# Second expert mixture: 64-row second blocks in float32 on two column halves of the matrix array

## The chip, the cores and the metric

The kernel runs on one core of a Trainium2 chip. The core has a matrix engine (TensorE, PE in the rows), VectorE (DVE), ScalarE (ACT), GpSimd (POOL) and SyncE (SP), which issues loads, and 16 DMA engines. The metric is the device time of one execution in microseconds (us), as the median of several runs. Lower is better.

## The reference, cut to what matters

A first transformer block is followed by a second one. The second ends in a mixture of 64 experts, of which each of the 1024 tokens takes 8, plus one shared expert:

```python
def moe_ffn(h, w_router, router_bias, w_gate, w_up, w_down, ws_gate, ws_up, ws_down):
    ...                                   # scores, the 8 experts of a token, their weights wts
    def block_ffn(args):                  # one block of rows xb of one expert e
        xb, e = args
        return (jax.nn.silu(xb @ w_gate[e]) * (xb @ w_up[e])) @ w_down[e]
    ...                                   # every row scaled by its wts and summed per token
    shared = (jax.nn.silu(xt @ ws_gate) * (xt @ ws_up)) @ ws_down
    return (routed + shared).reshape(B, S, D)
```

`w_gate[e]` and `w_up[e]` are 1024 x 256, `w_down[e]` is 256 x 1024, all float32: 3 MB an expert, 192 MB in all. They are read once.

## The kernel before

`experts` (L1389) runs a list of blocks. A block is up to 128 token rows of one expert. In the second mixture `moe2` (L2530) makes the list: five blocks of the shared expert, then the 64 routed experts, ranked by how many tokens they got, and three more shared blocks. `CAPS2` (L2528) gives the places an expert has by its rank: 4 experts have 224 rows (blocks of 128 and 96), 8 have 192 (128 and 64), 20 have 176 (128 and 48), and 32 have 128, one block. Ranks i and 63 - i follow each other, so that the stage is 32 *triples*: a first block of 128 rows, a second block, and the one block of a small expert.

There are two ways to multiply. For an expert of one block (`whole`) the loaded float32 weights are the moving operand as they lie in their place `raw`, and TensorE runs them as float32 (L1477, one matmul instruction in the program, two in the trace). For an expert of two blocks the weights are first split by `wsplit` (L1437) into a high part `gh`/`dh` and a rest `gl`/`dl`, in six pieces; a piece is a ScalarE copy and a VectorE subtraction (L247, L253). Each product is then three cheaper passes, `gh*xh`, `gl*xh`, `gh*xl` (`mm3`, L271 to L273). The stationary operand is the transposed block of rows, so that a block of R rows uses R of the array's 128 columns, and 512 weight columns stream by.

For each block the loop at the end of `experts` writes, in this order: the gate and up products into `gups`; up to three pieces of the next split; the activation (`act`: `th` on ScalarE, `hh` twice on VectorE); the down products `yps` of the block before (`down`), whose rows are scaled and added to the output in memory by an indirect DMA (`acc_d<-y`); the rest of the pieces; the transposes `tp` of the block after the next; the transpose `hT` of this block's activation; and a few small matmuls `tab` (L1492), which turn a one-hot matrix `oh` into the row numbers and weights of a later block. No scheduler moves these: each engine takes its instructions in the order written.

Weights are loaded in thirds (gate and up in two, down in one) of 1 MB into a pool of `RAW2 = 7` places `raw`. The load of a third is issued by SP when the third seven before it is free:

```python
            while len(raw) < min(3 * len(keys) if ready[0] else 3, freed[0] + RAW):
```

A third of a split expert is free once its two pieces are made (L1450), a third of a whole expert once its matmuls have run. `gh` and `gl` have two buffers of two tiles each, `dh` and `dl` one. The first mixture uses the same function with blocks of 96 rows and its own pools. `LEAD2` (L2617) says at which of the first blocks the pieces of the first routed expert stand; four of its six subtractions may go to GpSimd (L1448), as only the first two experts of the list are allowed to.

Of the kernel before, what the change touches and what calls it, by code (L numbers as in the profile page):

```python
# [231 lines left out]
class Body:  # L232
# [1156 lines left out]
    def experts(self, cx, blocks, xsrc, wsrc, acc_d, C, route, pre=None, fin=None, whole=lambda key: False):  # L1389
# [15 lines left out]
                keys.append(b[2])  # L1405
        uses = {k: sum(b[2] == k for b in blocks) for k in keys}
        last_of = {b[2]: n for n, b in enumerate(blocks)}
        Wt = {}

        RAW = self.RAW1 if pre else self.RAW2  # L1410
# [25 lines left out]

        def wsplit(i):  # L1437

            gh, gl = [[wp.tile([128, 2048], F32R, name=f"{n}{a}") for a in range(2)] for n in ("gh", "gl")]
            Wt[keys[i]] = W = [list(zip(gu(gh), gu(gl))), None]  # L1440
            for q in range(6):
                if q == 4:
                    dh, dl = [wp.tile([128, 2048], F32R, name=n, bufs=self.DBUFS[n0 > 0]) for n in ("dh", "dl")]
                    W[1] = list(zip(down_(dh), down_(dl)))
                c = slice(q % 2 * 1024, q % 2 * 1024 + 1024)
                h, lo = (gh[q // 2], gl[q // 2]) if q < 4 else (dh, dl)
                self.split(raw[3 * i + q // 2][:, c], h[:, c], lo[:, c],
                           lo_eng="pool" if i < 2 and q not in (self.LOD if i else self.LOD0)[n0 > 0] else "dve")  # L1448
                if q % 2:
                    free(3 * i + q // 2)  # L1450
                yield

# [17 lines left out]
        def products_(out, pairs, start=True, stop=True):  # L1470
# [5 lines left out]
            for i, (x, w) in enumerate(pairs):  # L1476
                nc.tensor.matmul(out, x, w, start=start and i == 0, stop=stop and i == len(pairs) - 1, **kw)  # L1477

        idx, ohs, tab = {}, {}, {}

        def onehot(n, oh=None):
            r, off = blocks[n][:2]
            oh = ohs[n] = ep.tile([128, 8, C], BF, name="oh") if oh is None else oh
            nc.vector.tensor_tensor(oh, self.slot_r[:, None, off:off + C].to_broadcast([128, 8, C]),
                                    self.pos[:, :, r:r + 1].to_broadcast([128, 8, C]), op=OP.is_equal)

        def tabmm(n, first, a=0, b=6):
            if n == first and a == 0:
                tab[0] = p1.tile([128, 8, 6], F32, name="tab")
            oh = ohs.pop(n) if b == 6 else ohs[n]  # L1490
            for t in range(8):
                nc.tensor.matmul(tab[0][:C, n - first, a:b], oh[:, t], self.cols[:, t, blocks[n][0], a:b],  # L1492
                                 start=n == first and t == 0 and a == 0, stop=t == 7, skip_group_check=True)

        def tabfin(first, size, a=0, b=6):
            s = (slice(0, C), slice(0, size))
            if a == 0:
                tab[1] = ep.tile([128, 8, 6], F32, name="tb")
            tb = tab[1]
            nc.vector.tensor_copy(tb[s][:, :, a:b], tab[0][s][:, :, a:b])  # L1500
            if a:
                w = idx[first][3]
                nc.vector.tensor_tensor(w[s], tb[s][:, :, 3], tb[s][:, :, 4], op=OP.add)
                nc.vector.tensor_tensor(w[s], w[s], tb[s][:, :, 5], op=OP.add)
                return
            gi, si = [ep.tile([128, 8], I32, name=n, bufs=4) for n in ("gi", "si")]
            w, e = [ep.tile([128, 8], F32, name=n, bufs=4) for n in ("wsl", "emp")]
            nc.vector.scalar_tensor_tensor(e[s], tb[s][:, :, 0], 128.0, tb[s][:, :, 1], op0=OP.mult, op1=OP.add)
            nc.vector.tensor_copy(gi[s], e[s])
            nc.vector.tensor_scalar(w[s], tb[s][:, :, 2], -1.0, 1.0, op0=OP.mult, op1=OP.add)  # L1510
            nc.vector.scalar_tensor_tensor(si[s], w[s], self.spare[:C], e[s], op0=OP.mult, op1=OP.add)
            if b == 6:
                nc.vector.tensor_tensor(w[s], tb[s][:, :, 3], tb[s][:, :, 4], op=OP.add)
                nc.vector.tensor_tensor(w[s], w[s], tb[s][:, :, 5], op=OP.add)
            for j in range(size):
                R = blocks[first + j][3]
                idx[first + j] = (gi[:R, j:j + 1], si[:R, j:j + 1], w[:R, j:j + 1], w)


        todo = {}  # L1520
# [38 lines left out]
        def trans(n):  # L1559
            if n >= N:  # L1560
                return
            xg, R = XG.pop(n), blocks[n][3]
            ps = p1.tile([128, 2, 512], F32, name="tp")
            for k in range(8):
                nc.tensor.transpose(ps[:, k // 4, (k % 4) * R:(k % 4) * R + R], xg[:R, k * 128:k * 128 + 128],  # L1565
                                    self.ident[:R, :R])
            pv = ps[:, :, :4 * R].rearrange("p a (k c) -> p a k c", k=4)
            v = lambda z: z.rearrange("p (a k) c -> p a k c", a=2)
            if whole(blocks[n][2]):
                x = ep.tile([128, 8, C], F32, name="x", tag="xh")[:, :, :R]  # L1570
                nc.scalar.activation(v(x), pv, AF.Copy)
                X[n] = [x[:, k] for k in range(8)]
                return
            xh, xl = [ep.tile([128, 8, C], F32R, name=n_)[:, :, :R] for n_ in ("xh", "xl")]
            nc.scalar.activation(v(xh), pv, AF.Copy)  # L1575
            nc.vector.tensor_tensor(v(xl), pv, v(xh).bitcast(F32), op=OP.subtract)  # L1576
            X[n] = [(xh[:, k], xl[:, k]) for k in range(8)]
# [3 lines left out]
        def gate_up(n, mid=None):  # L1581
            key, R = blocks[n][2:]
            ps = pg.tile([128, 512], F32, name="gups")
            ops = list(zip(X.pop(n), Wt[key][0]))
            if mid:
                products_(ps[:R], ops[:4], stop=False)
                mid()
                products_(ps[:R], ops[4:], start=False)
            else:
                products_(ps[:R], ops)  # L1590
            Hs[n] = ps
            if whole(key) and last_of[key] == n:
                free(3 * keys.index(key), 3 * keys.index(key) + 1)

        def act(n):
            ps, R = Hs[n], blocks[n][3]
            th = ep.tile([128, 256], F32, name="th")
            hh = ep.tile([128, 256], F32, name="hh")
            nc.scalar.activation(th[:R], ps[:R, 0:256], AF.Tanh, scale=0.5)  # L1599
            nc.vector.scalar_tensor_tensor(hh[:R], th[:R], 1.0, ps[:R, 0:256], op0=OP.add, op1=OP.mult)  # L1600
            nc.vector.tensor_tensor(hh[:R], hh[:R], ps[:R, 256:512], op=OP.mult)
            Hs[n] = hh

        def h_trans(n):
            hh, R = Hs[n], blocks[n][3]
            ps = p1.tile([128, 2, C], F32, name="hT")[:, :, :R]
            for k in range(2):
                nc.tensor.transpose(ps[:, k], hh[:R, k * 128:k * 128 + 128], self.ident[:R, :R])
            if whole(blocks[n][2]):
                h = ep.tile([128, 2, C], F32, name="hT", tag="hTh")[:, :, :R]  # L1610
                nc.scalar.activation(h, ps, AF.Copy, scale=0.5)
                Hs[n] = [h[:, k] for k in range(2)]
                return
# [6 lines left out]
        def down(n):  # L1620
# [2 lines left out]
            h, (key, R) = Hs.pop(n), blocks[n][2:]  # L1623
            while piece(keys.index(key)):
                pass
            if n < N - 1 or not fin:
                ps = p1.tile([128, 1024], F32, name="yps")
                ps = [ps[:, q * 512:q * 512 + 512] for q in range(2)]
            else:
                ps = [pg.tile([128, 512], F32, name="gups") for q in range(2)]  # L1630
# [84 lines left out]
        transposes(0 if not n0 else 1)  # L1715

        first_of = {b[2]: n for n, b in reversed(list(enumerate(blocks)))}
        plan, since = {}, 0
        for i, key in enumerate(keys[1:], 1):
            if whole(key):  # L1720
                continue
            if i > 1 or not n0:
                w = range(since, first_of[key])
                for q in range(6):
                    plan.setdefault(w[q * len(w) // 6], []).append((i, q))
            since = last_of[key]
        if n0:
            plan |= self.LEAD2
        for n in range(N):
            key = blocks[n][2]  # L1730
            ki = keys.index(key)
# [176 lines left out]
        return f  # L1908

    CAP1 = 96  # L1910
    RAW1, RAW2 = 7, 7
    DBUFS = 2, 1
    START, ORDER = (1, 1, 2, 0), "oswsSSx"
    YACT = 5
# [610 lines left out]
        yield  # L2525


    CAPS2 = [(4, 224), (8, 192), (20, 176), (32, 128)]  # L2528

    def moe2(self, rt):  # L2530
        nc, tc, IN = self.nc, self.tc, self.IN
# [13 lines left out]
        R = {}  # L2545
        blocks = [(None, t, "shared", C) for t in range(8 - self.NT)]
        for i in range(E // 2):
            for r in (i, E - 1 - i):
                blocks += [(r, o, r, min(C, cap[r] - o)) for o in range(0, cap[r], C)]
        blocks += [(None, t, "shared again", C) for t in range(8 - self.NT, 8)]  # L2550
        ws = self.wsrc("_2")
# [41 lines left out]
        def norms():  # L2593
            with tc.tile_pool(reuse_waits="tile", name="c2", bufs=2) as ep:
# [18 lines left out]
    NT = 3  # L2613
    ROUTE = {(-1, 0): 2, (-1, 1): 1, (-1, 2): 1, (-1, 3): 1, (0, 0): 1, (0, 1): 2, (0, 3): 1, (1, 1): 1, (1, 2): 1,
             (1, 3): 1, (2, 1): 1, (2, 2): 1, (5, 3): 1}

    LEAD2 = {2: [(1, 0), (1, 1)], 3: [(1, 2), (1, 3)], 5: [(1, 4), (1, 5)]}  # L2617

    def run(self):
        tc, nc = self.tc, self.nc  # L2620
# [88 lines left out]
```

## Time and profile before

| | us |
|---|---|
| median of 3 runs | 3308.56 (3307.82 to 3311.86) |
| the profiled execution | 3307.24 |
| its span in the trace | 3305.3 |
| TensorE busy | 3000.4 (91%) |
| VectorE / ScalarE / GpSimd busy | 2045.1 / 1394.6 / 1022.6 |
| mean granted TensorE clock | 0.952 |

The trace is of one execution. Busy time is the time in which an engine had an instruction under way; the ends of matmuls are modelled, so a TensorE that is busy throughout may still hold small gaps, and the distance from one start to the next is the surer price. The second mixture's routed experts lie from about 2240 us to 3226 us. The DMA share is the mean busy share of the core's 16 DMA engines.

### The profile page before, as it was taken

The page shows a single profiled execution, that of the slowest core. Times are in us where ns is not written, and L with a number is a line of the kernel's source. Part 1 is how long each engine was busy: PE and PEld are TensorE (multiplying, and loading weights), DVE is VectorE, ACT ScalarE, POOL GpSimd, SP SyncE. Part 2 cuts the span into 40 slices and gives each one's busy share as a digit, 9 for nine tenths or more (in the row PEclk, how much of TensorE's full clock was granted, in tenths as well). Part 3 has the DMA queues.
Part 4 walks back from the last instruction along what each step waited for, and adds up shares of the span by engine and source line. Part 5 has one row for each costly group of instructions (what it writes and reads, how often), then busy time and mean ns, then how long its engine had stood idle before and what let it go on. Part 6 is the DMA issues. An engine that isn't in the chain of part 4 may idle for free.

```text
span 3305.3 us, 43066 instructions
## 1 busy us (share of the span) xinstructions
PE 3000.4 (91%) x16001; PEld 2322.3 (70%) x16001; DVE 2045.1 (62%) x3146; ACT 1394.6 (42%) x2096; POOL 1022.6 (31%) x682
## 2 busy tenths in 40 slices
PE   5999999988888978998699999779999999999994
PEld 4778887987777876666588888756666666666663
DVE  5554651667777658998545665466655555555546
ACT  3332331536666326676434334423433333333332
POOL 0000000236777323563111331133333233333323
PEclk9999999998999988999899998889999999999997
DMA  3112120453332448999501004448999999999993
GB/s 111 64 58 76 64 86 8 134 169 82 90 86 75 160 167 274 345 346 348 179 29 37 26 4 138 147 157 248 289 288 301 280 279 297 276 281 297 282 275 131
DMA packets 225254, 577.17 MB, mean 175 GB/s; under 512 B 22421, under 2 KB 104005, under 8 KB 225013
## 3 DMA queue, kind: packets, MB, share of 16 engines
q1 hardware_dynamic: 188240, 445.42, 38.6%
q0 software_dynamic: 36368, 128.88, 16.3%
q8 instruction: 128, 2.10, 0.3%
q14 instruction: 86, 0.70, 0.1%
q10 hardware_dynamic: 432, 0.06, 0.0%
HBM read 468.90 MB, written 105.33 MB: 174 GB/s over the span
## 4 chain that ended last, share of the span: by engine, by line
PE 48%; DVE 13%; DMA 6%; issue 4%; ACT 3%; POOL 1%; SPq 0%; another core or an unknown queue 0%; DVEq 0%; POOLq 0%; ACTq 0%
PE gups L1477 7%; PE gups L273 4%; PE gups L271 4%; PE gups L272 4%; PE yps L1477 3%; PE tp L1565 2%; DVE gl L253 2%; PE yps L273 2%; PE yps L271 2%; PE yps L272 2%; PE mm L2196 2%; PE mm L2198 2%; PE mm L2197 2%; PE o L969 2%; PE mm L272 1%
## 5 line engine op out<-in xcount | busy, mean ns | idle before, releaser
L1648 POOL DMA_INDIRECT acc_d<-y,si x96 | 179.7, 1872 | 643.8 <-DVE y L1645 605.2
L271 PE MATMUL gups<-gh,xh 128*96 128x512 f32 (+3 forms) x832 | 344.0, 413 | 1.3 <-ACT xh L1575 0.9
L272 PE MATMUL gups<-gl,xh 128*96 128x512 f32 (+3 forms) x832 | 334.4, 402 | 11.6 <-DVE gl L253 11.6
L273 PE MATMUL gups<-gh,xl 128*96 128x512 f32 (+3 forms) x832 | 334.8, 402 | 0.4 <-DVE xl L1576 0.4
L271 PE MATMUL mm<-uh,wh 128*128 128x512 f32 x640 | 253.7, 396 | 10.8 <-ACT t L505 8.8
L273 PE MATMUL mm<-uh,wl 128*128 128x512 f32 x640 | 252.4, 394 | 0.0
L272 PE MATMUL mm<-ul,wh 128*128 128x512 f32 x640 | 251.7, 393 | 0.0
L1645 DVE TENSOR_SCALAR y<-yps,wsl 128x512 f32<-128x512 f32 (+3 forms) x123 | 91.9, 747 | 239.7 <-ACT y L1643 239.7
L1477 PE MATMUL gups<-raw,x 128*128 128x512 f32 x512 | 228.0, 598 | 0.0
L1599 ACT ACTIVATE th<-gups 128x256 f32<-128x256 f32 (+1 forms) x136 | 51.7, 380 | 412.7 <-PE gups L273 241.5
L253 POOL TENSOR_TENSOR pl<-raw,ph 128x1024 fp32r<-128x1024 f32 (+7 forms) x128 | 203.5, 1608 | 71.4 <-ACT ph L247 36.8
L1643 ACT ACTIVATE y<-yps,wsl 48x512 f32<-48x512 f32 (+2 forms) x128 | 87.7, 685 | 317.7 <-PE yps L273 218.2
L253 DVE TENSOR_TENSOR gl<-raw,gh 128x1024 fp32r<-128x1024 f32 x183 | 218.9, 1238 | 3.4 <-ACT gh L247 3.2
L247 ACT ACTIVATE gh<-raw 128x1024 fp32r<-128x1024 f32 x188 | 188.0, 1057 | 2.0 <-DMA raw<-in_w_up_dram 1.6
L272 PEld LDWEIGHTS gups<-gl,xh 128*96 128x96 f32 (+3 forms) x832 | 139.9, 168 | 65.0 <-issue 12.8
L273 PEld LDWEIGHTS gups<-gh,xl 128*96 128x96 f32 (+3 forms) x832 | 138.8, 167 | 60.8 <-DVE xl L1576 1.1
L271 PE MATMUL yps<-dh,hTh 128*96 128x512 f32 (+3 forms) x412 | 176.2, 428 | 3.8 <-ACT et L2506 2.3
L271 PEld LDWEIGHTS gups<-gh,xh 128*96 128x96 f32 (+3 forms) x832 | 139.3, 167 | 54.0 <-ACT xh L1575 1.2
L1477 PEld LDWEIGHTS gups<-raw,x 128*128 128x128 f32 x512 | 94.7, 190 | 108.8 <-issue 107.1
L273 PE MATMUL yps<-dh,hTl 128*96 128x512 f32 (+3 forms) x412 | 162.7, 395 | 0.0
L272 PE MATMUL yps<-dl,hTh 128*96 128x512 f32 (+3 forms) x412 | 162.1, 394 | 0.0
L1600 DVE SCALAR_TENSOR_TENSOR hh<-th,gups 128x256 f32<-128x256 f32 (+1 forms) x136 | 56.6, 416 | 163.3 <-ACT th L1599 162.4
(672 smaller groups left out, 8010.3 us busy)
## 6 DMA issues: line engine op xcount, KB each, us to landing
raw<-in_w_down_dram SPq DMA_DIRECT2D x78, 1024.0 KB, 8.5
raw<-in_w_gate_dram SPq DMA_DIRECT2D x154, 512.0 KB, 5.3
raw<-in_w_up_dram SPq DMA_DIRECT2D x154, 512.0 KB, 9.2
w<-in_w_in_dram SPq DMA_DIRECT2D x20, 1024.0 KB, 5.3
b<-in_w_gate_dram SPq DMA_DIRECT2D x38, 512.0 KB, 10.6
b<-in_w_up_dram SPq DMA_DIRECT2D x38, 512.0 KB, 12.5
b<-in_w_down_dram SPq DMA_DIRECT2D x18, 1024.0 KB, 12.8
w<-in_w_in_dram SPq DMA_DIRECT2D x20, 512.0 KB, 4.6
```

What stands on the lines that cost most here:

```text
L247: nc.scalar.activation(hi, src, AF.Copy)
L253: e.tensor_tensor(lo, src, hi.bitcast(F32), op=OP.subtract)
L271: nc.tensor.matmul(out, lh, rh, start=start and i == 0, stop=False, **kw)
L272: nc.tensor.matmul(out, lh, rl, start=False, stop=False, **kw)
L273: nc.tensor.matmul(out, ll, rh, start=False, stop=stop and i == n - 1, **kw)
L969: nc.tensor.matmul(O[h][a // 512][:, a % 512:a % 512 + b - a], v, p[:, sl], start=kt == 0 and i == 0, stop=kt == (7 if a >= 512 else 3) an ...
L1477: nc.tensor.matmul(out, x, w, start=start and i == 0, stop=stop and i == len(pairs) - 1, **kw)
L1565: nc.tensor.transpose(ps[:, k // 4, (k % 4) * R:(k % 4) * R + R], xg[:R, k * 128:k * 128 + 128], self.ident[:R, :R])
L1643: nc.scalar.activation(y[:R, 0:512], ps[0][:R], AF.Copy, scale=w)
L1645: nc.vector.tensor_scalar(y[:R, 512:1024], ps[1][:R], w, None, op0=OP.mult)
L1648: nc.gpsimd.indirect_dma_start(out=acc_d, out_offset=bass.IndirectOffsetOnAxis(ap=si, axis=0), in_=y[:R], in_offset=None, compute_op=OP.add)
L2196: nc.tensor.matmul(out, lh, rh, start=(i == 0), stop=False)
```

## The change

Second blocks of 64 rows (`half`) get a third way to multiply. The rows' transposed block is placed twice in the array, in columns 0 to 63 and 64 to 127 (`tile_position`). For gate and up each half streams 256 of the 512 weight columns (128 of gate, 128 of up), for down 512 of the 1024, all in float32 from `raw`. The outputs of the two halves lie on partitions 0 to 63 and 64 to 127. The activation then works on 128 x 128, its transpose is one instruction, and the `tab` matmuls of such a block run once for each half, since the row weights are needed on both. `CAPS2` gives 28 experts 192 places, so that 28 second blocks have 64 rows and none has 48. The raw thirds of such an expert are free only after its second block's matmuls; `RAW2` is 11, and `gh`, `gl` have one buffer instead of two. The one-block expert of a pair now comes first in the list, the pieces of a split may begin right after the last block that uses the split before, and `LEAD2` is gone.

```diff
+        split_to = {b[2]: n for n, b in enumerate(blocks) if b[0] is None or b[3] != 64}
...
-            gh, gl = [[wp.tile([128, 2048], F32R, name=f"{n}{a}") for a in range(2)] for n in ("gh", "gl")]
+            gh, gl = [[wp.tile([128, 2048], F32R, name=f"{n}{a}", bufs=self.DBUFS[n0 > 0]) for a in range(2)]
+                      for n in ("gh", "gl")]
...
-                if q % 2:
+                if q % 2 and last_of[keys[i]] == split_to[keys[i]]:
                     free(3 * i + q // 2)
...
+        def half(n):
+
+            return blocks[n][0] is not None and blocks[n][3] == 64
+
+        def products2(ps, xs, ws):
+
+            for i, (x, w) in enumerate(zip(xs, ws)):
+                for h in range(2):
+                    nc.tensor.matmul(ps[64 * h:64 * h + 64], x, w(h), start=i == 0, stop=i == len(xs) - 1,
+                                     skip_group_check=True, tile_position=(0, 64 * h))
...
+            W = 64 if half(n) else C
+            nc.vector.tensor_tensor(oh[:, :, :W], self.slot_r[:, None, off:off + W].to_broadcast([128, 8, W]),
+                                    self.pos[:, :, r:r + 1].to_broadcast([128, 8, W]), op=OP.is_equal)
...
+                for h in range(2 if half(n) else 1):
+                    p, kw = (slice(64 * h, 64 * h + 64), dict(tile_position=(0, 64 * h))) if half(n) else (slice(C), {})
+                    nc.tensor.matmul(tab[0][p, n - first, a:b], oh[:, t, :p.stop - (p.start or 0)],
...
+            if half(n):
+                j = 3 * keys.index(key)
+                products2(ps[:, 0:256], X.pop(n), [lambda h, w=w: w[:, :, 128 * h:128 * h + 128]
+                                                   for w in gu([raw[j], raw[j + 1]])])
+                Hs[n] = ps
+                if last_of[key] == n:
+                    free(j, j + 1)
+                return
...
+            if half(n):
+                ps = p1.tile([128, 1024], F32, name="yps")[:, 0:512]
+                j = 3 * keys.index(key) + 2
+                products2(ps, h, [lambda q, w=w: w[:, q * 512:q * 512 + 512] for w in down_(raw[j])])
+                if last_of[key] == n:
+                    free(j)
...
-        plan, since = {}, 0
+        plan, since = {}, split_to[keys[0]] if n0 else 0
...
+            w = range(since, first_of[key])
+            if n0 and i > 2 and len(w) > 2:
+                w = w[1:]
+            for q in range(6):
+                plan.setdefault(w[q * len(w) // 6], []).append((i, q))
+            since = split_to[key]
...
-    RAW1, RAW2 = 7, 7
+    RAW1, RAW2 = 7, 11
...
-    CAPS2 = [(4, 224), (8, 192), (20, 176), (32, 128)]
+    CAPS2 = [(4, 224), (28, 192), (32, 128)]
...
-            for r in (i, E - 1 - i):
+            for r in (E - 1 - i, i):
```

TensorE in a triple before, from the end of a first block to the small expert's products. `gups` are gate and up products, `yps` down products, `tp` and `hT` transposes; the last number pair is the shape of the output; rows left out repeat the pattern.

```order
L1608 MATMUL hT<-ident,hh 128x128 x2
...
L273 MATMUL gups<-gh_21295,xl 64x512
L271 MATMUL yps<-dh,hTh 128x512
L272 MATMUL yps<-dl,hTh 128x512
L273 MATMUL yps<-dh,hTl 128x512
...
L1565 MATMUL tp<-ident,xg 128x128 x8
...
L1608 MATMUL hT<-ident,hh 128x64 x2
L1477 MATMUL gups<-raw,x 128x512 x8
L271 MATMUL yps<-dh,hTh 64x512
```

The same stretch after the change:

```order
L1643 MATMUL hT<-ident,hh 128x128 x2
L1490 MATMUL gups<-raw,x 64x256 x16
L271 MATMUL yps<-dh,hTh 128x512
L272 MATMUL yps<-dl,hTh 128x512
L273 MATMUL yps<-dh,hTl 128x512
...
L1584 MATMUL tp<-ident,xg 128x128 x8
...
L1638 MATMUL hT<-ident,hh 128x128
L1480 MATMUL gups<-raw,x 128x512 x8
L1490 MATMUL yps<-raw,hT 64x512 x4
```

The second block's 24 passes for gate and up have become 16 float32 matmuls of 256 columns, its 12 passes for down 4 of 512 columns, and its two transposes of the activation one.

ScalarE in the same stretch before, from the first block's `hTh` on:

```order
L1616 ACTIVATE hTh<-hT 128x256
L247 ACTIVATE gh_24514<-raw 128x1024 x2
L247 ACTIVATE gh_24515<-raw 128x1024
L1599 ACTIVATE th<-gups 48x256
L1643 ACTIVATE y<-yps,wsl 128x512
L1575 ACTIVATE xh<-tp 128x1024
L1616 ACTIVATE hTh<-hT 128x2x48
```

and after:

```order
L1651 ACTIVATE hTh<-hT 128x256
L247 ACTIVATE gh_24402<-raw 128x1024 x2
L247 ACTIVATE gh_24403<-raw 128x1024
L1627 ACTIVATE th<-gups 128x128
L1691 ACTIVATE y<-yps,wsl 128x512
L1594 ACTIVATE xh<-tp 128x1024
L1646 ACTIVATE hT<-hT 128x2x64
```

The three pieces stand where they stood, ahead of the second block's `th`; the second block's activation is no longer split in two parts.

## Rows read from the trace of the kernel before

**Rows 1.** Windows: busy us of each engine (instructions), granted clock, DMA share, GB/s.

```profile
core 0: us, PE busy (x) PEld busy (x) DVE busy (x) ACT busy (x) POOL busy (x), PEclk, DMA share, GB/s
1330.00:1530.00 200.00, 182.72 (x972) 131.91 (x971) 189.33 (x242) 140.97 (x185) 117.44 (x38) 0.97 1.03 346
2368.00:3226.00 858.00, 858.00 (x4081) 535.35 (x4080) 480.50 (x670) 333.22 (x499) 272.01 (x163) 1.00 0.93 285
```

**Rows 2.** Timeline of TensorE: the small experts' gate and up products, 4th and 32nd.

```profile
2352.12 7.06 PE L1477 MATMUL gups<-raw,x 128*128 128x512 f32 x16
...
3216.45 7.13 PE L1477 MATMUL gups<-raw,x 128*128 128x512 f32 x16
```

**Rows 3.** Timeline of TensorE, one triple: start, us, instruction (array rows*columns, moving shape).

```profile
2620.11 0.47 PE L271 MATMUL gups<-gh,xh 128*48 128x512 f32 x1
...
2625.56 0.40 PE L273 MATMUL gups<-gh,xl 128*48 128x512 f32 x1
2625.79 0.39 PE L271 MATMUL yps<-dh,hTh 128*128 128x512 f32 x1
...
2628.55 1.03 PE L1565 MATMUL tp<-ident,xg 128*128 128x128 f32 x8
2629.42 0.34 PE L1492 MATMUL tab<-cols,oh 128*128 128x6 bf16 x8
2629.70 0.32 PE L1608 MATMUL hT<-ident,hh 48*128 48x48 f32 x2
```

**Rows 4.** Chain of work in order of time, same stretch: start, us, engine and line.

```profile
2615.59 3.43 PE yps L1477 x8
...
2629.76 0.25 PE hT L1608 x2
2630.02 7.06 PE gups L1477 x16
...
2639.87 0.62 PE tp L1565 x8
```

**Rows 5.** Groups by shape, 2368 to 3226 us: count | busy us, mean ns | idle before.

```profile
L271 PE MATMUL gups<-gh,xh 128*128 128x512 f32 x217 | 87.1, 401 | 0.0
...
L271 PE MATMUL gups<-gh,xh 128*48 128x512 f32 x160 | 65.1, 407 | 0.0
...
L271 PE MATMUL gups<-gh,xh 128*64 128x512 f32 x64 | 25.7, 402 | 0.0
```

**Rows 6.** DMA queues, 1330 to 1530 us (first mixture): packets, MB, share of 16 engines.

```profile
q1 hardware_dynamic: 14782, 54.84, 73.2%
q0 software_dynamic: 4044, 14.21, 29.7%
```

**Rows 7.** DMA queues, 2368 to 3226 us (second mixture).

```profile
q1 hardware_dynamic: 46920, 174.02, 56.3%
q0 software_dynamic: 19648, 69.68, 36.1%
```

**Rows 8.** SP's waits, 2368 to 3226 us: us in total, times, longest.

```profile
SPq L1926 <- PE gups L1477: 200.8, 27, 7.9
SPq L1926 <- DVE dl L253: 149.7, 27, 6.0
SPq L1923 <- PE yps L1477: 129.9, 27, 4.9
SPq L1923 <- DVE gl L253: 128.1, 27, 5.3
```

**Rows 9.** Timeline of ScalarE and VectorE beside the 48-row block.

```profile
2621.12 2.95 ACT L247 ACTIVATE gh<-raw 128x1024 fp32r<-128x1024 f32 x3
2625.99 0.38 ACT L1599 ACTIVATE th<-gups 48x256 f32<-48x256 f32 x1 [1.92 <-PE gups L273]
...
2622.74 3.50 DVE L253 TENSOR_TENSOR gl<-raw,gh 128x1024 fp32r<-128x1024 f32 x3
2626.40 0.41 DVE L1600 SCALAR_TENSOR_TENSOR hh<-th,gups 48x256 f32<-48x256 f32 x1 [0.16 <-ACT th L1599]
2626.85 0.41 DVE L1601 TENSOR_TENSOR hh<-hh,gups 48x256 f32<-48x256 f32 x1
```

More of the change, by code (lines that the diff above doesn't have):

```diff
@@ L1483, in onehot @@
             oh = ohs[n] = ep.tile([128, 8, C], BF, name="oh") if oh is None else oh
-            nc.vector.tensor_tensor(oh, self.slot_r[:, None, off:off + C].to_broadcast([128, 8, C]),
-                                    self.pos[:, :, r:r + 1].to_broadcast([128, 8, C]), op=OP.is_equal)
+            W = 64 if half(n) else C
+            nc.vector.tensor_tensor(oh[:, :, :W], self.slot_r[:, None, off:off + W].to_broadcast([128, 8, W]),
+                                    self.pos[:, :, r:r + 1].to_broadcast([128, 8, W]), op=OP.is_equal)
         def tabmm(n, first, a=0, b=6):
@@ L1491, in tabmm @@
             for t in range(8):
-                nc.tensor.matmul(tab[0][:C, n - first, a:b], oh[:, t], self.cols[:, t, blocks[n][0], a:b],
-                                 start=n == first and t == 0 and a == 0, stop=t == 7, skip_group_check=True)
+                for h in range(2 if half(n) else 1):
+                    p, kw = (slice(64 * h, 64 * h + 64), dict(tile_position=(0, 64 * h))) if half(n) else (slice(C), {})
+                    nc.tensor.matmul(tab[0][p, n - first, a:b], oh[:, t, :p.stop - (p.start or 0)],
+                                     self.cols[:, t, blocks[n][0], a:b],
+                                     start=n == first and t == 0 and a == 0, stop=t == 7, skip_group_check=True, **kw)
         def tabfin(first, size, a=0, b=6):
@@ L1516, in tabfin @@
                 R = blocks[first + j][3]
-                idx[first + j] = (gi[:R, j:j + 1], si[:R, j:j + 1], w[:R, j:j + 1], w)
+                idx[first + j] = (gi[:R, j:j + 1], si[:R, j:j + 1],
+                                  w[:, j:j + 1] if half(first + j) else w[:R, j:j + 1], w)
         todo = {}
@@ L1568, in trans @@
             v = lambda z: z.rearrange("p (a k) c -> p a k c", a=2)
-            if whole(blocks[n][2]):
+            if whole(blocks[n][2]) or half(n):
                 x = ep.tile([128, 8, C], F32, name="x", tag="xh")[:, :, :R]
@@ L1598, in act @@
             hh = ep.tile([128, 256], F32, name="hh")
-            nc.scalar.activation(th[:R], ps[:R, 0:256], AF.Tanh, scale=0.5)
-            nc.vector.scalar_tensor_tensor(hh[:R], th[:R], 1.0, ps[:R, 0:256], op0=OP.add, op1=OP.mult)
-            nc.vector.tensor_tensor(hh[:R], hh[:R], ps[:R, 256:512], op=OP.mult)
+            R, W = (128, 128) if half(n) else (R, 256)
+            nc.scalar.activation(th[:R, :W], ps[:R, 0:W], AF.Tanh, scale=0.5)
+            nc.vector.scalar_tensor_tensor(hh[:R, :W], th[:R, :W], 1.0, ps[:R, 0:W], op0=OP.add, op1=OP.mult)
+            nc.vector.tensor_tensor(hh[:R, :W], hh[:R, :W], ps[:R, W:2 * W], op=OP.mult)
             Hs[n] = hh
@@ L1605, in h_trans @@
             hh, R = Hs[n], blocks[n][3]
[L1606 to L1609, printed above, removed]
+            ps = p1.tile([128, 2, C], F32, name="hT")
+            if half(n):
+                ps = ps[:, 0, :128]
+                nc.tensor.transpose(ps, hh[:, 0:128], self.ident)
+                ps = ps.rearrange("p (k c) -> p k c", k=2)
+            else:
+                ps = ps[:, :, :R]
+                for k in range(2):
+                    nc.tensor.transpose(ps[:, k], hh[:R, k * 128:k * 128 + 128], self.ident[:R, :R])
+            if whole(blocks[n][2]) or half(n):
                 h = ep.tile([128, 2, C], F32, name="hT", tag="hTh")[:, :, :R]
@@ L1625, in down @@
                 pass
+            if half(n):
+                ps = p1.tile([128, 1024], F32, name="yps")[:, 0:512]
[3 more added lines that the diff above has]
+                    free(j)
+                y = ep.tile([128, 1024], F32, name="y")
+                _, si, w, _ = idx.pop(n)
+                nc.scalar.activation(y[:64, 0:512], ps[:64], AF.Copy, scale=w[:64])
+                nc.vector.tensor_scalar(y[:64, 512:1024], ps[64:128], w[64:128], None, op0=OP.mult)
+                nc.gpsimd.indirect_dma_start(out=acc_d, out_offset=bass.IndirectOffsetOnAxis(ap=si, axis=0),
+                                             in_=y[:64], in_offset=None, compute_op=OP.add)
+                return
             if n < N - 1 or not fin:
@@ L1721, in experts @@
                 continue
[L1722 to L1728, printed above, removed]
+            w = range(since, first_of[key])
[4 more added lines that the diff above has]
+            since = split_to[key]
         for n in range(N):
@@ L2615 @@
              (1, 3): 1, (2, 1): 1, (2, 2): 1, (5, 3): 1}
-    LEAD2 = {2: [(1, 0), (1, 1)], 3: [(1, 2), (1, 3)], 5: [(1, 4), (1, 5)]}
     def run(self):
```

## Prediction

> **What bounds the kernel now.** I looked first at the busy time by stretch. From 2368 to 3226 us, where 28 of the 32 triples of the second mixture run, TensorE is busy for 858.00 of 858 us at a granted clock of 1.00, its upper level of 2.4 GHz; VectorE has 480.50, ScalarE 333.22 and GpSimd 272.01 us there [rows 1]. No wait of TensorE is listed in that stretch, and the chain that ended last runs along TensorE there [rows 4]. So the stage is as long as its matmuls. The gate and up products of the fourth small expert start at 2352.12 us, those of the 32nd at 3216.45 us [rows 2]: 28 triples in 864.33 us, 30.87 us each. All 28 have a second block of 64 or 48 rows, and the change reaches only these.
>
> A second resource stands close behind. The DMA share of the stage is 0.93 [rows 1]. How full that is shows in the first mixture: from 1330 to 1530 us the share is 1.03 and TensorE is busy for 182.72 of 200 us, so there the DMA engines set the pace. The waits of SP say what holds loads back in the second mixture now: it waits for matmuls and splits to set places free [rows 8], not for DMA engines. With TensorE faster, the DMA engines are next, and the sum needs both.
>
> **What the second block costs now.** Its gate and up passes start at 2620.11 and the next products at 2625.79 us: 24 passes, 5.68 us [rows 3]. Its down passes run from the end of the small expert's products (2630.02 + 7.06 = 2637.08 us) to the transposes at 2639.87 us: 12 passes, 2.79 us [rows 4]. Together 8.47 us. The number of rows does not matter: passes of 128, 64 and 48 rows take 401, 402 and 407 ns [rows 5], so half of the array or more lies idle, and widening 20 blocks from 48 to 64 rows costs TensorE nothing.
>
> **What it costs after.** In float32 the small expert needs 7.06 us for 8 steps of 512 columns and 3.43 us for 4 [rows 4]: 0.883 us for gate and up, 0.858 us for down, and half of it for 256 columns. Gate and up: 8 steps x 2 halves x 0.441 us = 7.06 us one behind the other, 3.53 us side by side. Down: 2 steps x 2 halves x 0.858 us = 3.43 or 1.72 us. So 10.49 us if the halves take turns, 5.25 us if they stream together. No row of this trace shows two matmuls in the array at one time; the sum stands or falls with it. I take side by side: the halves share no column and no output partition, a pass of 64 rows leaves the other 64 columns without work [rows 5], and eight small `tab` matmuls follow each other in 0.28 us (2629.42 to 2629.70 [rows 3]), so that issuing 32 half-width instructions in 3.53 us is no limit. That gives 8.47 - 5.25 = 3.22 us saved.
>
> The Trainium skill says the same of the halves (TensorEngine Tiling (Array Packing), Key Properties: tiles operate independently and can load weights and multiply in parallel). It also has a rule against this change, in the same place: changing the tiling mode drains the engine.
>
> **What comes on top, per triple.** A drain is bounded by rows: a pass lasts 0.40 us, but the next starts after 5.68 / 24 = 0.237 us, so about 0.16 us of each hides under the next [rows 3]. The change switches between whole and half columns six times a triple (into and out of gate and up, down, `tab`): 0 if nothing drains, 6 x 0.16 = 1.0 us if each does; I take 0.5. The `tab` matmuls of the second block double: 0 to 0.56 us, I take 0.28 [rows 3]. One transpose `hT` instead of two saves half of 0.25 us, 0.12 [rows 4]. TensorE's triple: 30.87 - 3.22 + 0.5 + 0.28 - 0.12 = **28.31 us**, with ends at 30.87 - 3.22 - 0.12 = 27.53 and 29.1 us. By the page's rule on drains alone the sum would be 28.8 us; no run here shows a drain.
>
> **The DMA engines' triple.** The two queues that count take 56.3 + 36.1 = 92.4% of 30.87 us [rows 7], 28.5 us. Sixteen more rows, 4 KB in and 4 KB out each, are 0.131 MB at 0.361 x 858 us / 69.68 MB = 4.4 us a MB, 0.58 us for 20 of 28 triples, 0.42 on average: 28.9 us. In the full stretch of the first mixture the same two queues reach 73.2 + 29.7 = 102.9% [rows 6], so 28.9 / 1.029 = **28.1 us** is what the engines can do. With the prices of that stretch (0.732 x 200 / 54.84 = 2.67 and 0.297 x 200 / 14.21 = 4.18 us a MB, for 6.26 and 2.60 MB) it would be 27.6 / 1.029 = 26.8 us; without any overlap 28.9 us. The two limits are 0.2 us apart, and two such limits do not hide each other's unevenness: I take **28.7 us**, 0.4 above the larger.
>
> **What hides the rest.** The raw places cost nothing, I think. A split expert now holds its three places for about a triple, so that 8 of 11 serve the loads ahead, against 7 before, of which a split freed each third at once. `gh`, `gl` with one buffer: the first piece of the next split stands behind the second block's gate and up, and the first block, the last to read the old pieces, is done a down product and a transpose earlier. The three pieces still stand ahead of the second block's `th` on ScalarE and `hh` on VectorE. Today `gl` ends at 2626.24 us and `hh` at 2627.26, 2.4 us ahead of `hT` at 2629.70 [rows 3, 9]. With gate and up 2.15 us shorter `hT` comes 1.9 to 2.2 us earlier, and `hh`, of half the size, a little earlier: a cover of 0.2 to 0.5 us is left. If it is gone, each triple pays a few tenths. SP and GpSimd issue the same loads, gathers and scatters in the same order, but for the exchanged ranks.
>
> The start: the first routed block is now a small expert that needs no split, and the first split is made four pieces in a row on VectorE, under the 7.06 us of that block; I take 0. The end: the last shared split now stands beside a first and a second block instead of a second and a small one, and its first pieces wait for the first block to leave `gh`; 2 us.
>
> **The sum.** 28 x (30.87 - 28.7) = 60.8 us, less 2: 3307.24 - 58.8 = 3248.4 us for the profiled execution, which lies 1.3 us under the median of the runs: **3250 us**. The ends of the two triples, 27.5 and 29.4 us, give 3217 and 3269.
>
> **The rivals.**
> - *The DMA engines take over.* The share of 0.93 speaks for it, the 102.9% of the first mixture and eight places ahead against it. At 28.9 to 29.4 us a triple, middle 29.2: 28 x 1.67 - 2 = 45 us saved, 3264 us. TensorE would then wait for loads.
> - *The halves overlap only in part.* If each of the 10 steps of a second block leaves 0.16 us uncovered, the triple is 28.31 + 1.6, about 30.0 us: 3286 us. The Trainium skill bears on it (TensorE: Matmul & The Clock Gate, Measured speedup vs the span model: three column tiles run 2.38 times as fast as one); as an estimate from that page a pair would need 6.6 us instead of 5.25, which is 3277 us. No run here shows it.
> - *The halves take turns.* Nothing in the trace excludes it, since it shows no two matmuls at once. The second block then costs 10.49 instead of 8.47 us, the triple 28.31 + 5.24 = 33.55 us, and the kernel 28 x 2.68 + 2 = 77 us more: **3386 us**, slower. It decides from the point where the pair needs more than 5.25 + (30.87 - 28.31) = 7.8 us, that is where less than half of the second stream is covered.
> - *It doesn't do what it says*: the overlap is there but something else keeps the triple at 30.8 us, say an activation that comes late. VectorE's 480.50 us of 858 speak against it [rows 1].
>
> **How the numbers follow.** Forecast 0.48, DMA bound 0.20, partial overlap 0.11, in turns 0.16, no effect 0.05. A measurement of this kernel tells a change of 0.2%, 6.6 us, from none. Faster holds the first three, 0.79, less a little for the last ones' tails: 0.78; same 0.04; slower 0.18. The range leaves out the turns and a little at both ends: 3215 to 3300 us.
>
> **What would show it.** In the trace after, the two halves' float32 matmuls would have starts in pairs with 8 steps in about 3.5 us, against 7.1 us in turns; small experts' products would start 28.7 us apart; the DMA share would be 0.98 or more at over 300 GB/s; SP's waits for places would shrink, and a few waits of TensorE for loads or `hh` would appear. Eight steps in over 6 us would make the prediction wrong, and so would a triple over 30 us with pairs that do overlap.

## The result, and the profile after

The changed kernel takes **3259.3 us** (median of 4 runs, 3250.99 to 3262.36), the kernel before 3308.19 (3307.1 to 3311.86): a ratio of 0.9846, 95% interval 0.9827 to 0.9866. The profiled execution took 3259.96 us, with a span of 3258.1. In what follows a *period* is the time from one small expert's gate and up to the next one's, one triple.

Busy time by stretch of the kernel after (the columns of [rows 1]): the first 14 and the last 12 steady periods.

```profile
2415.00:2809.00 394.00, 394.00 (x2262) 244.65 (x2259) 228.73 (x323) 167.69 (x253) 130.68 (x84) 1.00 0.99 318
2809.00:3155.00 346.00, 339.26 (x1854) 207.44 (x1854) 186.75 (x261) 143.40 (x216) 98.25 (x72) 1.00 0.98 309
```

Against [rows 1], the DMA share went from 0.93 to 0.98 and 0.99, the rate from 285 to 318 and 309 GB/s, at the same clock. TensorE has no gap in the first stretch and 6.74 us of gaps in the second.

Timeline of TensorE after, as [rows 3]: start, duration, instruction.

```profile
2632.50 3.67 PE L1490 MATMUL gups<-raw,x 128*64 128x256 f32 x32
2636.10 0.50 PE L271 MATMUL yps<-dh,hTh 128*128 128x512 f32 x1
2636.44 0.39 PE L272 MATMUL yps<-dl,hTh 128*128 128x512 f32 x1
```

The second block's 32 half matmuls start at 2632.50 us, the next product at 2636.10: 3.60 us. So the halves do stream side by side; in turns it would be 7.06. One by one in the trace, the 32 starts come in 16 pairs, the two of a pair 5 to 8 ns apart, in all 28 second blocks.

The chain of work in order of time, as [rows 4], one triple on:

```profile
2640.36 6.87 PE gups L1480 x16
2647.23 1.87 PE yps L1490 x8
2649.09 0.64 PE tp L1584 x8
2649.74 0.35 PE tab L1509 x16
2650.08 0.37 PE hT L1643 x2
...
2660.43 0.28 PE hT L1643 x2
2660.72 3.60 PE gups L1490 x32
2664.32 0.43 PE yps L271
2664.74 0.23 PE yps L272
```

Down takes 1.87 us. The first pass after a half block takes 0.43 us instead of 0.23: the switch to whole columns costs 0.20 us there. Behind the half `tab` matmuls the two transposes `hT` take 0.37 us instead of 0.28.

The start of the second mixture is where time was lost. Waits of TensorE for rows of shared blocks, 2110 to 2330 us before, then 2090 to 2330 us after (total, times, longest):

```profile
PE tp L1565 <- DMA xg<-h_d: 3.0, 1, 3.0
```

```profile
PE tp L1584 <- DMA xg<-h_d: 27.7, 2, 15.8
```

SP's instructions before, from the first load of the shared expert's weights on (start, us, place, load):

```profile
2112.24 0.48 SPq L1923 DMA_DIRECT2D raw<-in_ws_gate_dram  x1
...
2123.16 0.33 SPq L1923 DMA_DIRECT2D raw<-in_ws_gate_dram  x1
...
2191.65 0.33 SPq L1553 DMA_DIRECT2D xg<-h_d  x1
```

The same after:

```profile
2109.99 0.49 SPq L1970 DMA_DIRECT2D raw<-in_ws_gate_dram  x1
...
2139.15 0.33 SPq L1970 DMA_DIRECT2D raw<-in_ws_gate_dram  x1
...
2213.43 0.33 SPq L1572 DMA_DIRECT2D xg<-h_d  x1
```

The second third of the shared weights is asked for 29.16 us after the first instead of 10.92, and the rows of the fifth shared block 103.4 us after it instead of 79.4. The first routed block starts 148.80 us after the first load (2258.79 - 2109.99) instead of 123.46 (2235.70 - 2112.24).

The balance, in spans: the 28 periods from the 4th to the 32nd small expert take 799.59 us (2355.30 to 3154.89) against 864.33 [rows 2], 64.7 less; the start costs 25.3; the first three triples and the end give 5.6; work ahead of the mixture, untouched, was 2.2 shorter. Together 47.2 us = 3305.3 - 3258.1. The periods don't hold quite the same blocks: the small expert of a pair comes first now, so the first two periods after (30.81 and 29.05 us) still hold products of a 96-row block, and the last half blocks lie behind the 32nd small expert, in the 5.6 us. The other 26 take 28.45 us on average.

### The profile page after: what moved, and what is told of

Read it like the earlier page. It is cut to its first block, busy times and chain, and to the rows that moved or that the text cites. A ratio compares the mean times of both kernels' runs of the same rounds, so it can differ in the third digit from the quotient of the medians.

```text
span 3258.1 us, 43717 instructions
## 1 busy us (share of the span) xinstructions
PE 2923.7 (90%) x16309; PEld 2268.3 (70%) x16309; DVE 2002.5 (61%) x3093; ACT 1395.4 (43%) x2096; POOL 988.0 (30%) x678
## 5 line engine op out<-in xcount | busy, mean ns | idle before, releaser
L272 PE MATMUL gups<-gl,xh 128*128 128x512 f32 (+1 forms) x608 | 246.9, 406 | 10.4 <-DVE gl L253 10.4
L271 PE MATMUL gups<-gh,xh 128*128 128x512 f32 (+1 forms) x608 | 254.5, 419 | 1.3 <-ACT xh L1594 0.9
L273 PE MATMUL gups<-gh,xl 128*128 128x512 f32 (+1 forms) x608 | 246.7, 406 | 0.4 <-DVE xl L1595 0.4
L1584 PEld LDWEIGHTS tp<-ident,xg 128*128 128x128 f32 (+2 forms) x1088 | 112.5, 143 | 97.2 <-issue 36.4
L1584 PE MATMUL tp<-ident,xg 128*128 128x128 f32 (+2 forms) x1088 | 128.2, 261 | 42.2 <-DMA xg<-h_d 27.7
L1693 DVE TENSOR_SCALAR y<-yps,wsl 128x512 f32<-128x512 f32 (+1 forms) x95 | 71.1, 748 | 137.5 <-ACT y L1691 137.5
L271 PEld LDWEIGHTS mm<-uh,wh 128*128 128x128 f32 x640 | 121.8, 190 | 38.0 <-ACT t L505 10.6
L272 PEld LDWEIGHTS gups<-gl,xh 128*128 128x128 f32 (+1 forms) x608 | 112.2, 184 | 43.1 <-issue 11.8
L273 PEld LDWEIGHTS mm<-uh,wl 128*128 128x128 f32 x640 | 121.6, 190 | 25.7
L272 PEld LDWEIGHTS mm<-ul,wh 128*128 128x128 f32 x640 | 121.7, 190 | 25.4
```

What stands on the lines that cost most here:

```text
L271: nc.tensor.matmul(out, lh, rh, start=start and i == 0, stop=False, **kw)
L272: nc.tensor.matmul(out, lh, rl, start=False, stop=False, **kw)
L273: nc.tensor.matmul(out, ll, rh, start=False, stop=stop and i == n - 1, **kw)
L1693: nc.vector.tensor_scalar(y[:R, 512:1024], ps[1][:R], w, None, op0=OP.mult)
```

## The experiments

Times to compare with: before 3308, after 3259.3.

**The overlap itself.** A half's matmuls are issued in other orders: all steps of one half first, then two by two, then four by four (one execution each).

```diff
-            for i, (x, w) in enumerate(zip(xs, ws)):
-                for h in range(2):
+            for h in range(2):
+                for i, (x, w) in enumerate(zip(xs, ws)):
```

> The changed kernel, except that a second block's matmuls run all steps of one column half and then all steps of the other, the same instructions in another order. Theory A (the gain of the change is that neighbouring instructions of the two halves stream at the same time): with neighbours in the same half they take turns, gate and up take 7.06 us instead of 3.6, down 3.43 instead of 1.9, the triple 28.1 + 5.0 = 33.1 us, and the time is 28 x 5 = 140 us more, less what the DMA engines gave away: about 3380 to 3400, slower than the kernel before. Rival (float32 at 64 columns is cheap by itself, or the engine reorders): the time stays near 3259. Between: one half's last step overlaps the other's first only, 0.4 us of gain a block.

It took 3324.65 us, slower than before, but not the 3380 to 3400 of theory A. The chain:

```profile
2610.47 1.88 PE yps L1490 x8
...
2623.96 6.25 PE gups L1490 x32
```

Gate and up go from 3.60 to 6.25 us and the period from 28.13 to 30.78, the same 2.65 us. So the gain hangs on the overlap. But 6.25 is not 7.06, and down, now four matmuls of one half and then four of the other, still takes 1.88: some overlap is left. Windows from the first of these 32 matmuls on, gate and up alone, with the number begun until each window's end:

```profile
2623.88:2626.52 2.64, 2.63 (x12) 1.00 0.96 312
2623.88:2627.44 3.56, 3.55 (x20) 1.00 1.04 311
2623.88:2629.84 5.96, 5.95 (x32) 1.00 1.01 260
```

Twelve matmuls begin in 2.64 us, 0.22 us each, the next eight in 0.92 us, and the last twelve in 2.40 us. So the other half starts when four of the first half's 16 are left. A look-ahead of about four matmuls would fit, and gives numbers for groups of four and eight:

> The changed kernel, with the steps of the two halves taken two by two: two steps of one half (four matmuls in the trace), two of the other. With all steps of one half first, gate and up took 6.25 us and down still 1.87. Theory A (a half may run at most about four matmuls behind the issue, so the other half starts that far early: 28 x 0.22 = 6.2 us with 16 in a row, none lost with 4 in a row): gate and up 3.6 us, the triple 28.13 us, the time within 6 us of 3259. Rival B (only direct neighbours in the queue overlap, and down owes its 1.87 us to something else): of 4 in a row, 3 are uncovered, gate and up take 5.5 us or more, the triple 30 us.

> The changed kernel, with four steps of one half (eight matmuls in the trace), then four of the other. Theory A (about four matmuls of look-ahead): the second half starts after 4 of the first's 8, and each later group of 8 starts 4 after the one before: 20 x 0.22 = 4.4 us for gate and up, 1.87 for down, the triple 28.13 + 0.8 = 28.9 us, the time 10 to 20 us over 3259. Rival B (only neighbours overlap): gate and up 6.4 us, the triple 30.9. Rival C (the look-ahead is deeper and the 6.25 us has another cause): 3.6 us.

```diff
+            for j in range(0, len(xs), G):            # G = 2, then 4
+                for h in range(2):
+                    for i in range(j, min(j + G, len(xs))):
```

The chains, two by two and then four by four:

```profile
2613.93 3.65 PE gups L1491 x32
```

```profile
2621.07 4.63 PE gups L1491 x32
```

3.65 us at a period of 28.2 (3264.55 us in all), and 4.63 us at 29.17 (3287.9 us, 28.6 over 3259.3 and not the 10 to 20 expected). Only the look-ahead fits both. The number begun, four by four:

```profile
2620.98:2621.91 0.93, 0.91 (x4) 1.00 0.81 277
2620.98:2624.67 3.69, 3.67 (x28) 1.00 1.00 285
2620.98:2625.34 4.36, 4.34 (x32) 1.00 0.98 271
```

Four begin alone, 24 in the next 2.76 us, four alone. That is 20 steps of 0.216 us, as exactly four matmuls of look-ahead make it; the rest of the 4.63 us lies at the ends and at the changes of group. Start by start, all 28 second blocks show it: 4 alone, 12 pairs, 4 alone here, and 12 alone, 4 pairs, 12 alone with one half after the other.

**The start.** Two causes were possible. With 11 places SP issues 11 thirds ahead of the fifth shared block's rows, before 7; and in another pool layout the second place lies where the stage ahead still has a buffer in use. SP's wait at 2139 us after names a buffer of that stage (from 2105 to 2150 us):

```profile
SPq L1970 <- DVE xf L2419: 20.8, 1, 20.8
```

The first edit allows 7 places until those rows are asked for, the second gives three of the 11 places an address range of their own, the third does both.

```diff
-            while len(raw) < min(3 * len(keys) if ready[0] else 3, freed[0] + RAW):
+            while len(raw) < min(3 * len(keys) if ready[0] else 3, freed[0] + (7 if few[0] else RAW)):
...
+                if n == n0 - 1:
+                    few[0] = False
+                    pump()
```

> The changed kernel, except that only 7 thirds of weights may be ahead until the rows of the fifth shared block have been asked for; then 11. Theory A (a queue moved: the four more loads that 11 places let SP issue stand ahead of that block's rows): the wait of TensorE for these rows falls from 15.8 us to about 3, the first routed block starts some 13 us earlier after the first load of the shared weights (148.8 -> about 136 us), and the time falls by 13 us to about 3246. Rival B (the DMA engines are the bound of the whole stage): the rows come earlier, but the weights come no earlier, the triples take longer by as much, and the time stays within 4 us of 3259. Rival C (the other wait, 11.9 us for rows at the second shared block, grows by what this one loses): the start stays at 148 us.

```diff
-            return wp.tile([128, 2048], F32, name="raw", bufs=RAW)
+            turn[0] += 1
+            low = (turn[0] - 1) % RAW < 3
+            return wp.tile([128, 2048], F32, name="raw", tag="low" if low else "raw", bufs=3 if low else RAW - 3)
```

> The changed kernel, except that the first three of the 11 places have an address range of their own, low, where they lay with 7 places. Theory A (the second place of the shared expert lies where a buffer of the stage ahead is still in use, so its load waits, and the rows queued behind it on SP with it): the load of the second third is issued about 11 us after the first instead of 29, the wait of 11.9 us for rows at the second shared block goes, the first routed block starts 10 to 12 us earlier, and the time falls by about 11 us to 3248. The 15.8 us wait stays, or grows a little. Rival B (DMA bound): start earlier, time within 4 us of 3259. Rival C (the address is no cause: SP waits for something else): the load is issued as late as now and nothing moves.

> Both edits together. Theory A: start at about 124 to 126 us after the first shared load, as in the kernel before (123.7), instead of 148.8; the time falls by 23 to 25 us, to 3234 to 3237. Rival B (DMA bound stage gives it back): 3255 to 3262. Between them: the second half of the stage, where triples take 28.8 instead of 28.1 us, gives back part, 3240 to 3250.

Measured: 3241.24 us (ratio to before 0.9809, 0.979 to 0.9828), 3246.49 (0.9816, 0.9801 to 0.9831) and **3236.72** (0.9789, 0.9775 to 0.9802). TensorE's waits for these rows, first edit, second edit, both:

```profile
PE tp L1588 <- DMA xg<-h_d: 11.7, 1, 11.7
```

```profile
PE tp L1590 <- DMA xg<-h_d: 17.9, 1, 17.9
```

```profile
PE tp L1594 <- DMA xg<-h_d: 1.9, 1, 1.9
```

With the second edit the second third is asked for 11.6 us after the first again. Each edit takes away one of the two waits, and the first routed block starts 131.5, 137.1 and 122.9 us after the first load. The medians fall by 18.1, 12.8 and 22.6 us, the starts came 17.3, 11.7 and 25.9 us earlier. So the start was lost time, and nearly all that is saved there arrives in the total: with both edits 3.3 us less than that, no more than the spread of the runs, though the DMA share is 1.00. The first edit gained more than the 13 us expected.

**The late triples.** The 14 periods from 2415.17 to 2809.00 us take 28.13 us each, the 12 from there to 3154.89 us 28.82. Waits of GpSimd and of TensorE from 2809 to 3155 us after:

```profile
POOL acc_d L1696 <- DMA acc_d<-y,si: 91.7, 12, 8.9
POOL acc_d L1671 <- DMA acc_d<-y,si: 55.9, 7, 9.1
```

```profile
PE tp L1584 <- DMA xg<-h_d,gi: 6.7, 9, 1.8
```

Of the 36 scatter-adds there, 19 are listed as waiting for the one before to land, up to 9.1 us, and a gather of rows stands behind each in GpSimd's order. The kernel before lists one such wait from 2368 to 3226 us (8.7 us). To tell this chain from full DMA engines, the second blocks' scatters were sent to another tensor, so that two a triple remain in the chain:

```diff
-                nc.gpsimd.indirect_dma_start(out=acc_d, out_offset=bass.IndirectOffsetOnAxis(ap=si, axis=0),
+                nc.gpsimd.indirect_dma_start(out=self.h_d, out_offset=bass.IndirectOffsetOnAxis(ap=si, axis=0),
```

> The changed kernel, except that the scatters of the 64-row second blocks add into another tensor, so that they no longer stand in the chain of scatters into the output (the second blocks' rows are left out of the result). The changed kernel's 12 last triples took 28.82 us on average against 28.13 before them. Theory A (three scatter-adds of some 9 us each, one after the other, are as long as the triple; gathers stand behind them on GpSimd and TensorE waits for rows): with two a triple in the chain and one outside it, GpSimd's waits for a scatter to land all but go, the late triples take 28.13 us, and the time falls by 8 to 10 us to about 3250. Rival B (the DMA engines, at a share of 0.98 to 1.00, are simply full, and rows come late for that): GpSimd waits less, but the late triples still take 28.5 us or more and the time stays within 4 us of 3259.

It took 3253.35 us (3251.87 to 3255.43). The waits of GpSimd from 2812 to 3148 us, and that window:

```profile
POOL acc_d L1696 <- DMA acc_d<-y,si: 10.9, 2, 5.5
```

```profile
2812.00:3148.00 336.00, 336.00 (x1865) 207.97 (x1864) 187.03 (x261) 143.39 (x217) 117.10 (x72) 1.00 1.01 319
```

The 12 last periods take 27.96 us on average (2812.48 to 3147.98), TensorE has no wait, and this at a DMA share of 1.01. So full DMA engines did not make the late gaps, and with the chain cut they are gone. The 28 periods take 789.20 us instead of 799.59, 10.4 less; in this execution the mixture began 2.2 us later and its start took 1.2 us longer. The medians differ by 6 us, not 8 to 10, and the runs of the changed kernel spread over 11.

The chain's length alone does not set the loss. With three scatters a triple in the chain, the profiles of the first and second edit of the start have 28 periods of 792.34 and 794.61 us in all, though GpSimd's waits for scatters from 2400 to 3150 us are 163.8 and 259.7 us, against 198.3 in the changed kernel. A scatter that waits costs time only where a gather behind it comes too late for TensorE; why that happens more in one execution than in another stays open. In the version with both edits the last 12 periods take 28.36 us each (2788.51 to 3128.87). In one more run of that version each gather was written one block earlier:

```diff
-            gathers(n + 3)
+            gathers(n + 4 if n > n0 > 0 else n + 3)
```

> The version with both edits of the start, with each gather of rows written one block earlier in GpSimd's queue, so that it stands behind one scatter-add fewer. Theory A (the late triples of over 28.13 us come from gathers behind a scatter that waits for the one before it): TensorE's waits for gathered rows go, and the time falls by the 3 to 5 us that its triples lost, to about 3232. Rival B (the DMA engines are full, or the scatters then come later by as much): the waits stay, and the time is within 2 us of 3237. Rival C (the earlier gathers take DMA time ahead of the weights): waits for weights appear, slower than 3240.

3236.65 us (3228.62 to 3243.43; ratio to before 0.9778, 0.976 to 0.9796): the same median as without it, but two of the five executions took 3229 us and three 3237 to 3243. The profile is of one of 3241.29 us. TensorE's waits for rows from 2400 to 3150 us, and a scatter on GpSimd some 12 us ahead of the longest, with its own wait in brackets:

```profile
PE tp L1594 <- DMA xg<-h_d,gi: 7.7, 3, 6.7
```

```profile
2868.98 1.44 POOL L1681 DMA_INDIRECT acc_d<-y,si  x1 [9.78 <-DMA acc_d<-y,si]
```

In this execution the earlier place in the queue didn't take the wait away; what the two shorter ones did, no trace shows.

**The places.** Both edits of the start, with 8 places:

```diff
-    RAW1, RAW2 = 7, 11
+    RAW1, RAW2 = 7, 8
```

> The version with both edits of the start, with 8 raw places instead of 11. Theory A of the prediction (three places of 11 are held by a split expert, 8 serve loads ahead, and that many are needed to keep the DMA engines fed): with 8, five are ahead, TensorE waits for loads, the DMA share falls to 0.95 or less, the triple goes from 28.13 to 29 us or more, and the time to over 3260. Rival B (places are not the limit, 7 were enough before): triples stay at 28.13 us and the time within 5 us of 3237.

3252.28 us (3247.91 to 3262.81), 15.6 more than with 11. Half of it is start again (130.6 instead of 122.9 us; the cause stays open); the 28 periods take 803.16 instead of 795.08 us. TensorE's wait that is longest in total from 2400 to 3150 us, and the chain at one long period, 31.23 us:

```profile
PE hT L1648 <- DVE hh L1639: 9.2, 11, 2.3
```

```profile
2616.28 8.83 DMA raw<-in_w_gate_dram
...
2625.20 1.07 ACT gh L247
...
2626.29 1.23 DVE gl L253
2627.51 0.21 DVE hh L1638
...
2627.75 0.30 DVE hh L1639
...
2628.18 0.30 PE hT L1648
```

A third comes late, the pieces of the split wait for it, and `hh` stands behind the pieces: this is the cover that the prediction priced at 0.2 to 0.5 us. The DMA share stayed at 1.00, against the 0.95 expected, the period is 28.68 us on average and not 29 or more, and the time stayed under 3260.

**The widening alone.** The kernel before with 28 second blocks of 64 rows, all in three passes.

```diff
-    CAPS2 = [(4, 224), (8, 192), (20, 176), (32, 128)]
+    CAPS2 = [(4, 224), (28, 192), (32, 128)]
```

> The kernel before, with 28 second blocks of 64 rows in place of 8 of 64 and 20 of 48, all in three passes as before: the widening alone. Theory A (the passes are as long for 64 rows as for 48, and the DMA engines have room at a share of 0.93): the triple stays at 30.87 us, the time within 5 us of 3308, the DMA share at 0.94 to 0.95. Rival B (16 more rows in and out cost the 0.42 us of DMA time a triple): 28 x 0.42 = 12 us more, about 3320.

3306.77 us, ratio 0.9995 (0.9986 to 1.0005): nothing. The window of [rows 1]:

```profile
2368.00:3226.00 858.00, 858.00 (x4090) 546.00 (x4089) 487.30 (x674) 336.82 (x501) 261.04 (x165) 1.00 0.95 289
```

TensorE is as full as before, the DMA share is 0.95 instead of 0.93. So none of the gain is the widening's, and the changed order of the halves' matmuls alone took all of it away (3324.65 us). The places and the exchanged ranks were not tried alone in the kernel before; TensorE had no idle time there that they could have saved [rows 1].

## Why the prediction was right, and where it was off

The time, 3259.3 us, lies 9 us over the forecast and inside the range; the mechanism was the predicted one, the two halves side by side. That the time came so close is in part luck: 25.3 us lost at the start and 13.7 us won elsewhere make up the 11.6 us between the sum and the profiled execution.

- **The second block.** 5.25 us were predicted, 3.60 + 1.87 = 5.47 were measured. Two of the six switches show a cost, 0.20 and 0.09 us, so the term of 0.5 us was not too small. The doubled `tab` cost 0.06 us (0.35 against 0.29 in the chain) and not 0.28. TensorE's triple was forecast at 28.31 us, and the undisturbed period is 28.13. The Trainium skill says that different tiles can multiply in parallel and that a change of mode drains the engine (TensorEngine Tiling (Array Packing), Key Properties). The trace agrees with the first by its 3.60 us, and shows a cost at two switches for the second. The rivals "partial overlap" and "in turns" fell; with one half after the other, gate and up come near to the second of them (6.25 of 7.06 us), down does not.
- **The DMA engines.** They were given 28.1 us a triple, close to TensorE's limit, and 0.4 us for unevenness. The mean of the 28 periods is 28.56 us, against 28.7. The size was right and the reason was not: 28.13 and less were kept at a share of 0.99 to 1.01, and what the late triples lost went away with the chain of scatter-adds cut. The prediction had priced the scatters as bytes and not as a chain. It ought to have been on the list: three scatters of 8 to 9 us each, as long as GpSimd waits for them now, are nearly a triple.
- **The start, "I take 0".** This is the mis-sized term: it cost 25.3 us. The sentence that failed is "SP and GpSimd issue the same loads, gathers and scatters in the same order". With 11 places SP has more loads to issue before the fifth shared block's rows, and places of another pool layout wait for other buffers. Two experiments priced the two causes at 18.1 and 12.8 us, both together at 22.6.
- **The end, 2 us.** The first three triples and the end were 5.6 us shorter instead, in part because the last half blocks lie there now.
- **"The raw places cost nothing."** True with 11 in the steady stage. With 8 the periods are 0.29 us longer, through the `hh` that was named as the cover. In the steady stage of the kernel after, TensorE lists no wait for `hh`, a split or a load of weights.
- **SP's waits** for places hardly shrank: 549 us in the five largest groups of 2368 to 3182 us, a share of 0.67, against 609 of 858 us in the four largest, 0.71 [rows 8].
- **The sum** for the profiled execution was 3248.4 and it took 3259.96: 25.3 for the start, -3.9 for the periods (64.7 instead of 60.8), -7.6 for the end and the first triples, -2.2 ahead, 11.6 in all.

One reading of the prediction is not borne out by the trace before: that in the first mixture "the DMA engines set the pace", from which the 102.9% and the 28.1 us came. From 1330 to 1530 us VectorE is busy for 189.33 of 200 us [rows 1]; what TensorE waited for longest, and SP:

```profile
PE hT L1608 <- DVE hh L1601: 12.1, 13, 3.2
```

```profile
SPq L1923 <- DVE dl L253: 51.5, 16, 6.2
SPq L1923 <- DVE gl L253: 50.8, 16, 6.8
```

These waits are for VectorE; for a transfer TensorE waited 0.3 us. So 102.9% was a share that was reached there, not a limit that was shown.

## What to carry to other kernels

A block of 64 rows can use both halves of the array at once, and then float32 beats three cheaper passes; write the two halves' matmuls alternately; four of one half in a row, as the trace counts them, cost next to nothing here (3.65 us against 3.60), eight did (4.63 us). When a pool grows, follow the issuing queue through the first loads: what is asked for earlier stands ahead of what is needed sooner, and an address that moved waits for whoever had it. A chain of scatter-adds, one after the other, can become a limit of its own: compare its latency times its count with the period, beside bytes and busy time.

## What the runs showed of the hardware

Matmuls of one half need not wait until all earlier matmuls of the other have begun. Runs of 2, 4, 8 and 16 matmuls of one half before the other's turn took 3.60, 3.65, 4.63 and 6.25 us for the same 32. If starts kept the written order, each run would overlap the next by one matmul at most, so runs of 4 would take about (32 - 7) x 0.22 = 5.5 us and runs of 16 (32 - 1) x 0.22 = 6.8. The Trainium skill says that starts and ends of packed matmuls keep program order strictly (TensorE: Matmul & The Clock Gate, Part 3: Packing small matmuls); these times don't fit that, and the measurement decides. The single starts give the depth: the other half's first matmul starts when four of a run of 8 or of 16 are left (2.64 us and 12 matmuls into the run of 16). Where the waiting matmuls are held, no row shows.

The DMA engines kept up at a share of 1.01 and 319 GB/s for 336 us without one wait of TensorE; a share near 1 was not by itself a bound there.
